# FFN up products on seeded sums in one whole-PSUM tile, with wide eviction and the last product one group later

## The chip, the cores and the metric

The kernel runs on one core of one Trainium2 chip. The metric is the device time of one execution in microseconds (us), the median of several runs. A core has five engines that work beside each other, each through its own queue in order: PE (TensorE, matmuls into PSUM), DVE (VectorE), ACT (ScalarE), POOL (GpSimd) and SP (SyncE, which here issues the DMAs). PSUM has eight banks of 128 x 512 numbers of 32 bits.

## The reference

One transformer layer for 1024 tokens of width 1024: a mixed attention and a recurrent (RWKV-7) branch, a gated merge and an output projection with a residual, and then the feed-forward part, which is where most of the change lies:

```python
def _conv_ffn(h, w_up, conv_w, w_down):
    u = h @ w_up
    u = lax.conv_general_dilated(u, conv_w[:, None, :], window_strides=(1,),
                                 padding=((CONV_WIDTH - 1, 0),),
                                 dimension_numbers=('NWC', 'WIO', 'NWC'),
                                 feature_group_count=u.shape[-1])
    a, b = jnp.split(u, 2, axis=-1)
    return (jax.nn.silu(a) * b) @ w_down
...
    x = x + y @ w_out[l]
    x = x + _conv_ffn(_rms_norm(x, norm_ffn[l]), ffn_up[l], ffn_conv[l], ffn_down[l])
```

`w_up` is 1024 x 5632, so `a` and `b` have 2816 = 22 x 128 columns each. The convolution has three taps along the tokens, one set per column.

## The kernel before, in words

Activations lie transposed: 128 features on the partitions, tokens along the free axis, in two halves of 512 tokens (half 0, half 1). Every large product is made from 16-bit parts: a 32-bit operand is split into a high part (ACT, a copy to 16 bits) and a low part (the rest, on DVE or POOL), and a product is the three matmuls high x high, high x low and low x high for each of the blocks of 128 along the contraction. Weights are scaled by 256 (`WS`) before the split; the convolution's weights carry 1/256.

The program is written with a tile framework: it places the tiles, sets the semaphores, and orders each engine's queue when the program is built, by priority and by a simulated time line. That order is fixed on the chip. A tile whose buffer is taken again waits until its former users are done; a new pool that lands on the bytes of closed pools waits, in the kernel before, for all the users of those pools. PSUM is eight tiles of one bank, drawn by `ps(tag)` (L214) from four pairs of banks P, M, A, B.

The stages, in order of time: normalization, projections and attention with fill-in projections (to about 620 us); the RWKV part, unit by unit, with dense fill-ins (to about 970), among them the output projection of half 0 (`wout0`, L822), its normalization `norm0` (L841) and the up part of half 0 for the first feature groups (`ffn0`, L868, i = 0 to 5); then half 1: projection, normalization, and the up part of half 1 for i = 0 to 5 (loop at L1618). In that loop, `wslot` (L1590) loads and splits weights, `taps` (L1512) evicts a bank, with ACT for the first tap and DVE for the two shifted ones, the first tokens of half 1 taking two columns of half 0 from `cvl`; `silu` (L1522) makes tanh on ACT and two gate steps on DVE and stores `th_d`. Beside it `tprep` (L1538) makes the 16 sums of normalized rows (T1 to T4) that the next stage needs; the rows of half 0 are there only as 16-bit pairs, and `summed` adds these up again.

For i = 6 to 21 both halves are done together in the loop at L1670 ("group" below). Its 2 x 2 block product (two halves of the contraction and a, b by two token halves) is made with seven products of 12 matmuls each in place of eight (Strassen's scheme in Winograd's form), on sums of weights and sums of rows. `prep_up` (L1600) prepares the next group's weights in four steps: load both raw tiles and scale them on ACT (`wraw`, L1573), split `a`; sums `s12` on DVE and their split; sums `s34` and their split; split of the second half of `b`. `split8` (L1580) takes the high part on ACT and the low part on POOL. The results are put together by five DVE sums over PSUM and two kept tiles (p1, q, u2); four evictions of 512 columns follow (L1688 to L1697), then two gates.

The down part follows (L1702 to the end), with the same kind of products; its weights pass `wraw` and `slot` (L1727).

The change and the prediction touch, by line: L81 (`HT`, tags of half 0's normalized rows), L178 to L184 (pools), L214 (`ps`), L841 (`norm0`), L1116 to L1121 (pools of the RWKV stage), L1507 to L1696 and L1727. L261 is the low part of `wload`, used by all the earlier weights; L271 and L291 are matmuls of the plain products, L1649 those of the grouped ones, L1759 and L1830 those of the down part.

## Time and profile before

| What | us |
|---|---|
| median of 3 runs (lowest, highest) | 1735.83 (1735.3, 1738.83) |
| the profiled execution, its own time | 1733.72 |
| its span, first to last instruction | 1731.9 |
| PE busy in it | 1646.6 |
| DVE busy | 1247.6 |
| ACT busy | 941.2 |
| POOL busy | 453.0 |
| first matmul of the grouped up products starts | 1180.4 |
| last row of them in the time line starts | 1510.66 |

The profile is of one execution. Matmuls are pipelined, so a busy PE is not a PE at its peak: the count of matmuls in a stretch says more than its busy time. In rows of groups, `out<-in` are the program's tile names without numbers; "count | busy us, mean ns | idle before" follow. In the chain of waits each row is a start, a length, and the engine, tile and line that the chain runs over there. PEld is the loading of weights, SPq the DMA issues of SP's queue.

### The profile page before, as it was taken

The page shows a single profiled execution, that of the slowest core. Times are in us where ns is not written, and L with a number is a line of the kernel's source. Part 1 is how long each engine was busy: PE and PEld are TensorE (multiplying, and loading weights), DVE is VectorE, ACT ScalarE, POOL GpSimd, SP SyncE. Part 2 cuts the span into 40 slices and gives each one's busy share as a digit, 9 for nine tenths or more (in the row PEclk, how much of TensorE's full clock was granted, in tenths as well). Part 3 has the DMA queues.
Part 4 walks back from the last instruction along what each step waited for, and adds up shares of the span by engine and source line. Part 5 has one row for each costly group of instructions (what it writes and reads, how often), then busy time and mean ns, then how long its engine had stood idle before and what let it go on. Part 6 is the DMA issues. An engine that isn't in the chain of part 4 may idle for free.

```text
span 1731.9 us, 30712 instructions
## 1 busy us (share of the span) xinstructions
PE 1646.6 (95%) x11856; PEld 862.9 (50%) x11856; DVE 1247.6 (72%) x2202; ACT 941.2 (54%) x1669; POOL 453.0 (26%) x350
## 2 busy tenths in 40 slices
PE   8999999999999999998999899998998999999998
PEld 3455555555555545675665444443443343444443
DVE  6446577778876656945447595698988888886799
ACT  6665675657667735446445563664544444546430
POOL 1101131121112210000103201103443333556756
PEclk9999999999999999999999999999999999999999
DMA  5342243242444465335455754443222222534402
GB/s 201 112 137 93 85 152 106 80 141 59 130 146 138 126 224 173 124 120 177 135 183 173 272 177 146 141 141 113 92 91 74 73 74 73 185 132 134 134 13 109
DMA packets 124691, 224.66 MB, mean 130 GB/s; under 512 B 16384, under 2 KB 45440, under 8 KB 124416
## 3 DMA queue, kind: packets, MB, share of 16 engines
q1 hardware_dynamic: 124544, 222.69, 39.0%
q8 instruction: 93, 1.52, 0.4%
q14 instruction: 54, 0.44, 0.1%
HBM read 153.86 MB, written 63.96 MB: 126 GB/s over the span
## 4 chain that ended last, share of the span: by engine, by line
PE 37%; DVE 19%; DMA 6%; ACT 5%; issue 3%; SPq 0%; POOL 0%; DVEq 0%; ACTq 0%
PE psP L271 10%; DVE u L1517 4%; DVE th L1527 3%; DMA wraw<-f_up 3%; PE psA L271 2%; PE psP L291 2%; PE psM L1759 1%; PE psP L1759 1%; PE psB L1759 1%; PE psM L1649 1%; PE psA L1759 1%; PE psM L271 1%; PE psP L1830 1%; DMA zs<-sg_d 1%; PE psA L1649 1%
## 5 line engine op out<-in xcount | busy, mean ns | idle before, releaser
L271 PEld LDWEIGHTS <-whi 128*128 128x128 f16 x1840 | 176.9, 98 | 209.7 <-issue 12.1
L271 PE MATMUL psP<-hlo,whi 128*128 128x512 f16 x560 | 212.2, 379 | 2.1 <-DVE hlo L246 2.1
L271 PE MATMUL psP<-hhi,whi 128*128 128x512 f16 x560 | 212.3, 379 | 2.0 <-ACT ad L973 1.5
L261 DVE SCALAR_TENSOR_TENSOR wlo<-wraw,whi 128x1024 f16<-128x1024 f32 (+1 forms) x98 | 112.0, 1143 | 62.5 <-ACT whi L259 38.2
L1577 ACT ACTIVATE wraw<-wraw 128x1024 f32<-128x1024 f32 x66 | 69.7, 1056 | 141.5 <-DMA wraw<-f_up 96.3
L664 DVE TENSOR_TENSOR pl<-pf,ph 128x512 f16<-128x512 f32 (+3 forms) x208 | 117.9, 577 | 36.0 <-ACT pf L663 35.3
L271 PE MATMUL psP<-hhi,wlo 128*128 128x512 f16 x560 | 142.3, 381 | 0.0
L259 ACT ACTIVATE whi<-wraw 128x1024 f16<-128x1024 f32 (+1 forms) x98 | 92.8, 949 | 90.5 <-PE psP L271 46.5
L271 PEld LDWEIGHTS <-wlo 128*128 128x128 f16 x920 | 88.0, 98 | 100.0 <-issue 4.3
L662 ACT ACTIVATE ph<-psA 128x512 f16<-128x512 f32 (+3 forms) x208 | 99.6, 479 | 63.7 <-PE psA L657 32.8
L599 DVE TENSOR_REDUCE mp<-psM 128x1 f32<-128x512 f32 (+2 forms) x192 | 96.0, 516 | 36.2 <-PE psM L597 27.1
L1585 POOL TENSOR_TENSOR wlo<-wraw,whi 128x1024 f16<-128x1024 f32 (+1 forms) x33 | 58.2, 1765 | 162.1 <-ACT whi L1584 146.8
L663 ACT ACTIVATE pf<-psA 128x512 f32<-128x512 f32 (+3 forms) x208 | 100.3, 482 | 0.0
L1527 DVE SCALAR_TENSOR_TENSOR th<-th,u 128x512 f32<-128x512 f32 x38 | 69.1, 1818 | 0.5
L1384 POOL TENSOR_TENSOR b<-b,bonus 128x512 f32<-128x512 f32 x8 | 10.5, 1317 | 217.1 <-ACT b L1382 189.1
L686 POOL TENSOR_TENSOR onat<-onat,ot 128x256 f32<-128x256 f32 x32 | 27.5, 863 | 140.2 <-DVE ot L685 107.2
L672 PEld LDWEIGHTS <-pl 128*128 128x128 f16 x592 | 55.9, 99 | 16.4 <-DVE pl L664 7.1
L667 PEld LDWEIGHTS <-ph 128*128 128x128 f16 x592 | 56.1, 97 | 16.1 <-ACT ph L662 3.1
L1649 PEld LDWEIGHTS <-whi 128*128 128x128 f16 x384 | 38.0, 99 | 49.2 <-issue 5.4
L1585 POOL TENSOR_TENSOR s34l<-s,s34h 128x1024 f16<-128x1024 f32 x16 | 34.6, 2164 | 101.1 <-ACT s34h L1584 101.1
L670 PEld LDWEIGHTS <-ph 128*128 128x128 f16 x592 | 56.2, 98 | 6.1 <-issue 1.9
L1649 PEld LDWEIGHTS <-s34h 128*128 128x128 f16 x256 | 25.7, 100 | 56.0 <-issue 29.2
(707 smaller groups left out, 4612.9 us busy)
## 6 DMA issues: line engine op xcount, KB each, us to landing
wraw<-f_up SPq DMA_DIRECT2D x56, 512.0 KB, 3.3
wraw<-w_t SPq DMA_DIRECT2D x46, 512.0 KB, 3.8
wraw<-f_dn SPq DMA_DIRECT2D x22, 512.0 KB, 3.8
th_d<-th SPq DMA_DIRECT2D x38, 256.0 KB, 2.1
sg_d<-zs SPq DMA_DIRECT2D x32, 256.0 KB, 2.6
wraw<-w_out SPq DMA_DIRECT2D x16, 512.0 KB, 3.3
z_d<-zs SPq DMA_DIRECT2D x28, 256.0 KB, 2.8
x<-xT SPq DMA_DIRECT2D x24, 256.0 KB, 5.8
```

Of the source, the lines that this page charges most:

```text
L259: A.activation(hi[:, :nk], raw, AF.Copy, scale=WS)
L261: V.scalar_tensor_tensor(lo[:, :nk], raw, WS, hi[:, :nk], op0=ALU.mult, op1=ALU.subtract)
L271: lastm[0] = T.matmul(ps, a[:, k], ks_(b, k), start=(n == 0), stop=(n == 3 * nk - 1)).ins
L599: V.reduce_max(mp[:, x, br, t:t + 1], pm[:, 0:(b1 - b0) * 128], axis=AX.X)
L662: A.activation(ph[0:nkey, rg], pa[0:nkey, rg], AF.Exp, scale=0.125)
L663: A.activation(pf[0:nkey, rg], pa[0:nkey, rg], AF.Exp, scale=0.125)
L664: V.tensor_sub(pl[0:nkey, rg], pf[0:nkey, rg], ph[0:nkey, rg])
L1517: V.scalar_tensor_tensor(u[:, d:512], pj[:, 0:512 - d], cw_, u[:, d:512], op0=ALU.mult, op1=ALU.add)
L1527: V.scalar_tensor_tensor(th, th, 0.5, ub, op0=ALU.mult, op1=ALU.mult)
L1577: A.activation(raw, raw, AF.Copy, scale=WS)
L1585: e.tensor_sub(lo[:, ks], raw[:, ks], hi[:, ks])
L1649: T.matmul(bank, w[wi][:, o_ + k], xs_[k][xi], start=start and n == 0, stop=n == 11, skip_group_check=True)
```

## The change

1. All pools get `reuse_waits="tile"`: a tile in a new pool waits only for the users of earlier tiles on its own bytes, not for all the users of the closed pools there.
2. PSUM is one tile of 4096 columns, and `ps` gives slices of 512 columns of it.
3. `norm0` keeps half 0's normalized rows in 32 bits: four in place in the residual tiles, four in a new pool g0; the 16-bit parts of the last two rows move to that pool. `tprep` reads these rows where it added pairs.
4. In the half-1 loop (i < 6) the tap of the first two columns becomes one add of a product made ahead (`edge`); weights whose low part DVE takes aren't scaled first, since the scale is part of the split; the first two are scaled on POOL.
5. `prep_up`: no scaling of raw weights, sums on POOL, low parts on DVE with the scale in the same operation; s12 and s34 splits have two buffers.
6. The loop of groups: ACT copies a partial sum into another bank, and the next product adds to it there (`start=False`); two full sets of four banks by turns; eviction over 1024 columns, both halves at once, so that no tap of half 0's last columns is needed; the last product with its eviction, gate and store (`last`) comes after the second product of the next group.
7. In the down part, the tags and buffers that follow from this.

```diff
-        pp = pool("ps", 1, PSUM)
+        pall = pool("ps", 1, PSUM).tile([128, 4096], F32, name="pall")
...
-            return pp.tile([128, 512], F32, name="ps" + tag, tag=f"bank{b[-1]}", bufs=1)
+            return pall[:, 512 * b[-1]:512 * b[-1] + 512]
...
+                src = t
+                if k < 4:
+                    t = FP["g"].tile([128, 512], F32, name=f"g0_{k}", tag=f"g0_{k}")
+                h2g[k] = t
...
-                    V.scalar_tensor_tensor(t, t, P("norm_ffn", k), rs, op0=ALU.mult, op1=ALU.mult)
+                    V.scalar_tensor_tensor(t, src, P("norm_ffn", k), rs, op0=ALU.mult, op1=ALU.mult)
...
+            V.tensor_tensor(edge[:, :, :, 0], cvl[:, :, :, 1], cw1, op=ALU.mult)
+            V.tensor_tensor(edge[:, :, :, 1], cvl[:, :, :, 0], cw2, op=ALU.mult)
+            V.tensor_add(edge[:, :, :, 0], edge[:, :, :, 0], edge[:, :, :, 1])
+            V.tensor_tensor(edge[:, :, :, 1], cvl[:, :, :, 1], cw2, op=ALU.mult)
...
-                if h:
-                    V.scalar_tensor_tensor(u[:, 0:d], prev(d), cw_, u[:, 0:d], op0=ALU.mult, op1=ALU.add)
+            if h:
+                V.tensor_add(u[:, 0:2], u[:, 0:2], edge[:, i, o])
...
-            t1 = diff(1, f12, summed(0, k), "fu")
+            t1 = diff(1, f12, h2g[k], "fu")
...
-            t4 = diff(4, summed(0, k + 4), t2, "yx")
+            t4 = diff(4, h2g[k + 4], t2, "yx")
...
+            if e is G:
+                lasts[0] = A.activation(hi[:, ks], raw[:, ks], AF.Copy).ins
+                G.tensor_sub(lo[:, ks], raw[:, ks], hi[:, ks])
+            else:
+                lasts[0] = A.activation(hi[:, ks], raw[:, ks], AF.Copy, scale=WS).ins
+                V.scalar_tensor_tensor(lo[:, ks], raw[:, ks], WS, hi[:, ks], op0=ALU.mult, op1=ALU.subtract)
...
         def prep_up(i):
-            ra, rb = wraw(D["f_up"][i]), wraw(D["f_up"][22 + i])
+            ra, rb = ((fp, wp)[i % 2].tile([128, 8, 128], F32, name="wraw", bufs=2) for _ in range(2))
+            load(ra, D["f_up"][i])
+            lastw[0] = load(rb, D["f_up"][22 + i]).ins
             w = {"a": split8(ra, wp, wp, "whi", "wlo", bufs=2)}
+            s12, s34 = (fp.tile([128, 8, 128], F32, name=n_) for n_ in ("s12", "s34"))
+            G.tensor_add(s12[:, lo4], rb[:, lo4], rb[:, hi4])
+            G.tensor_sub(s12[:, hi4], s12[:, lo4], ra[:, lo4])
             yield w
...
+            w["12"] = split8(s12, fp, fp, "s12h", "s12l", bufs=2)
+            G.tensor_sub(s34[:, lo4], ra[:, lo4], rb[:, lo4])
+            G.tensor_sub(s34[:, hi4], ra[:, hi4], s12[:, hi4])
+            yield
+            w["34"] = split8(s34, fp, fp, "s34h", "s34l", bufs=2)
...
+        def taps2(o, i, c):
+            ci = 22 * o + i
+            u = wide(f"U{o}")
+            A.activation(u, c, AF.Copy, scale=P("conv", 88 + ci))
+            for d in (1, 2):
+                V.scalar_tensor_tensor(u[:, d:1024], c[:, 0:1024 - d], P("conv", 44 * (2 - d) + ci), u[:, d:1024],
+                                       op0=ALU.mult, op1=ALU.add)
+            return u
...
+        def last(i, w, ua, cc):
+            b0 = cc[:, 0:512]
+            prod(b0, w["b"], 4, TB[4], False)
+            ub = taps2(1, i, cc)
+            th = wide("TH")
+            t_ = A.activation(th, ua, AF.Tanh, scale=0.5).ins
+            V.scalar_tensor_tensor(th, th, 1.0, ua, op0=ALU.add, op1=ALU.mult)
+            V.scalar_tensor_tensor(th, th, 0.5, ub, op0=ALU.mult, op1=ALU.mult)
+            for h in range(2):
+                nc.sync.dma_start(th_d[h][i], th[:, H[h]])
+            return t_
...
-            pa, pb, pc, pd_ = ps("P"), ps("M"), ps("A"), ps("B")
-            prod(pa, w["a"], 0, b11, True)
-            p1 = tmp("p1", "zs", NZS)
-            A.activation(p1, pa, AF.Copy)
-            prod(pb, w["12"], 4, TB[2], True)
-            u2 = tmp("u2", "fu", 3)
-            V.tensor_add(u2, pb, p1)
-            prod(pa, w["a"], 4, b21, False)
+            ca, cb_ = (pall[:, b_:b_ + 1024] for b_ in (1024 * (i % 2), 2048 + 1024 * (i % 2)))
+            a0, a1, b0, b1 = ca[:, 0:512], ca[:, 512:1024], cb_[:, 0:512], cb_[:, 512:1024]
+            prod(a0, w["a"], 0, b11, True)
+            A.activation(b0, a0, AF.Copy)
+            prod(b1, w["12"], 0, TB[1], True)
+            p5 = fp.tile([128, 512], F32, name="p5")
+            A.activation(p5, b1, AF.Copy)
+            if pend:
+                t_ = last(*pend)
+            prod(b0, w["12"], 4, TB[2], False)
+            A.activation(a1, b0, AF.Copy)
             wn = next(g_)
-            prod(pc, w["12"], 0, TB[1], True)
-            q = tmp("q", "fu", 3)
-            V.tensor_add(q, pc, p1)
+            prod(a0, w["a"], 4, b21, False)
             next(g_)
-            prod(pb, w["34"], 0, TB[3], False)
-            V.tensor_add(pd_, pb, q)
...
+            prod(b0, w["34"], 0, TB[3], False)
+            u3 = fp.tile([128, 512], F32, name="u3")
+            A.activation(u3, b0, AF.Copy)
+            V.tensor_add(b1, b1, u3)
+            prod(a1, w["34"], 4, b22, False)
+            V.tensor_add(a1, a1, p5)
+            pend = i, w, taps2(0, i, ca), cb_
             next(g_)
```

More of the change, by code (lines that the diff above doesn't have):

```diff
@@ L180, in pool @@
                 kw["space"] = space
-            return stack.enter_context(tc.tile_pool(name=name, bufs=bufs, **kw))
+            return stack.enter_context(tc.tile_pool(name=name, bufs=bufs, reuse_waits="tile", **kw))
         cp = pool("cst")
-        pp = pool("ps", 1, PSUM)
+        pall = pool("ps", 1, PSUM).tile([128, 4096], F32, name="pall")
         wp = pool("w")
@@ L323, in build @@
         cvl = cp.tile([128, NE, 2, 2], F32, name="cvl")
+        edge = cp.tile([128, NE, 2, 2], F32, name="edge")
         km_d = dr.tile([4, 128, S], F32, name="km_d")
@@ L839, in wout0 @@
                 ob["sq7"] = sq
+        h2g = [None] * 8
         def norm0():
@@ L852, in norm0 @@
             for n, k in enumerate(NK):
-                hi[k], lo[k] = (FP["h"].tile([128, 512], F16, name=f"h2{c}0_{k}", tag=HT[2 * n + x]) for x, c in enumerate("hl"))
+                hi[k], lo[k] = (FP["g" if n > 5 else "h"].tile([128, 512], F16, name=f"h2{c}0_{k}", tag=HT[2 * n + x])
+                                for x, c in enumerate("hl"))
                 if k > 3:
@@ L1507, in build @@
             tc.cur_priority = pe_ + 20000
+            cw1, cw2 = (par[:, o_:o_ + 44].rearrange("p (o i) -> p i o", o=2)[:, 0:NE]
+                        for o_ in (PAR["conv"][0] + 44, PAR["conv"][0]))
+            V.tensor_tensor(edge[:, :, :, 0], cvl[:, :, :, 1], cw1, op=ALU.mult)
+            V.tensor_tensor(edge[:, :, :, 1], cvl[:, :, :, 0], cw2, op=ALU.mult)
+            V.tensor_add(edge[:, :, :, 0], edge[:, :, :, 0], edge[:, :, :, 1])
+            V.tensor_tensor(edge[:, :, :, 1], cvl[:, :, :, 1], cw2, op=ALU.mult)
         yst.close()
@@ L1510, in build, with taps @@
         fp = pool("ffn", 1, stack=fst)
-        def taps(u, o, i, h, pj, prev):
+        def taps(u, o, i, h, pj):
             ci = 22 * o + i
@@ L1533, in utile @@
         def utile(o, h):
[L1534 removed]
+            return fp.tile([128, 512], F32, name=f"u{o}{h}", tag=f"U{o}", bufs=2)
         TB = [[None] * 4 for _ in range(5)]
         def tprep(k):
[L1539 to L1542 removed]
             def split(j, t):
@@ L1571, in build, with wraw, wslot @@
         rn_ = [3]
-        def wraw(src):
+        def wraw(src, scale="A"):
             rn_[0] += 1
-            raw = (wp, fp)[rn_[0] // 2 % 2].tile([128, 8, 128], F32, name="wraw", bufs=2)
+            x_ = rn_[0] // 2 % 2
+            raw = (wp, fp)[x_].tile([128, 8, 128], F32, name="wraw", bufs=2)
             lastw[0] = load(raw, src).ins
-            A.activation(raw, raw, AF.Copy, scale=WS)
+            if scale == "A":
+                A.activation(raw, raw, AF.Copy, scale=WS)
+            elif scale == "G":
+                G.tensor_scalar(raw, raw, WS, 0.0, op0=ALU.mult, op1=ALU.add)
             return raw
         def split8(raw, ph, pl, th, tl, ks=slice(0, 8), e=None, **kw):
-            e = e or G
             hi = ph.tile([128, 8, 128], F16, name=th, **kw)
             lo = pl.tile([128, 8, 128], F16, name=tl, **kw)
-            lasts[0] = A.activation(hi[:, ks], raw[:, ks], AF.Copy).ins
-            e.tensor_sub(lo[:, ks], raw[:, ks], hi[:, ks])
+            if e is G:
[4 more added lines that the diff above has]
+                V.scalar_tensor_tensor(lo[:, ks], raw[:, ks], WS, hi[:, ks], op0=ALU.mult, op1=ALU.subtract)
             return hi, lo
         wn_ = [0]
-        def wslot(src, ks=slice(0, 8)):
+        def wslot(src):
             n = wn_[0] % 4
@@ L1635, in build @@
                     run(mm3(pj, hi, lo, h2hi[1], h2lo[1], 8))
-                lasts[0] = taps(u, o, i, 1, pj, lambda d: cvl[:, i, o, 2 - d:2])
+                lasts[0] = taps(u, o, i, 1, pj)
                 us.append(u)
@@ L1663, in build, with wide @@
                     load(acc[m, h], x2_d[h][m])
-        def tmp(name, tag, n):
-            return FP["f"].tile([128, 512], F32, name=name, tag=tag, bufs=n)
+        def wide(name):
+            return fp.tile([128, 1024], F32, name=name, tag=name, bufs=2)
+        def taps2(o, i, c):
[6 more added lines that the diff above has]
+            return u
@@ L1680, in build @@
             wn = next(g_)
-            prod(pc, w["12"], 0, TB[1], True)
-            q = tmp("q", "fu", 3)
-            V.tensor_add(q, pc, p1)
+            prod(a0, w["a"], 4, b21, False)
             next(g_)
-            prod(pb, w["34"], 0, TB[3], False)
-            V.tensor_add(pd_, pb, q)
-            u = [[utile(o, h) for h in range(2)] for o in range(2)]
-            taps(u[0][0], 0, i, 0, pa, None)
-            prod(pc, w["34"], 4, b22, False)
+            prod(b0, w["34"], 0, TB[3], False)
@@ L1696, in build @@
-            t_ = taps(u[1][0], 1, i, 0, pb, None)
-            taps(u[1][1], 1, i, 1, pd_, lambda d: pb[:, 512 - d:512])
-            silu(i, 0, u[0][0], u[1][0])
-            silu(i, 1, u[0][1], u[1][1])
             w = wn
+        t_ = last(*pend)
         for m in range(4, 8):
@@ L1731, in slot @@
                 return [wp.tile([128, 8, 128], F16, name=t, bufs=2) for t in ("whi", "wlo")]
-            return [fp.tile([128, 8, 128], F16, name=t) for t in (("s12h", "s12l"), ("s34h", "s34l"))[n // 2]]
+            return [fp.tile([128, 8, 128], F16, name=t, bufs=2) for t in (("s12h", "s12l"), ("s34h", "s34l"))[n // 2]]
         def cut(dst, src, e):
```

34 lines of the change are left out of this document (10 added, 24 removed).

## The prediction, made before the changed kernel was timed

> **What bounds the kernel now.** I read the page first, then a table of busy time by stretches, then who PE waits for, then the chain of waits.
>
> ```profile
> span 1731.9 us, 30712 instructions
> ...
> PE 37%; DVE 19%; DMA 6%; ACT 5%; issue 3%; SPq 0%; POOL 0%; DVEq 0%; ACTq 0%
> ```
>
> ```profile
> 1180.41:1200.00 19.59, 13.35 (x51) 5.26 (x50) 19.20 (x33) 10.96 (x16) 6.63 (x3) 0.83 0.51 183
> 1200.00:1280.00 80.00, 80.00 (x372) 36.26 (x371) 67.76 (x106) 40.30 (x55) 34.74 (x18) 1.00 0.25 86
> 1280.00:1500.00 220.00, 198.88 (x881) 87.63 (x879) 188.65 (x263) 102.39 (x142) 84.71 (x44) 0.97 0.23 79
> ...
> 1100.00:1180.41 80.41, 80.41 (x373) 36.37 (x372) 76.18 (x119) 58.22 (x80) 10.85 (x4) 1.00 0.38 128
> 1514.98:1690.00 175.02, 175.02 (x811) 79.24 (x810) 136.95 (x191) 85.95 (x139) 113.28 (x85) 1.00 0.31 104
> ...
> 780.00:1000.00 220.00, 201.47 (x2100) 120.36 (x2099) 121.01 (x219) 116.11 (x204) 37.12 (x26) 0.97 0.58 192
> ```
>
> The columns are the stretch, its length, then busy time and instructions of PE, PEld, DVE, ACT and POOL, then the granted clock, DMA share and GB/s. The rewritten loop (i = 6 to 21, seven products each) runs from 1180.4 to about 1515. Its pace when nothing holds it is in the second row: 372 matmuls in 80.00 us, 0.215 us each, so 84 matmuls of one group are 18.1 us. Against that pace 1180 to 1200 loses 19.59 - 51 x 0.215 = 8.6 us, and 1280 to 1500 loses 220 - 881 x 0.215 = 30.6 us; the rows between, before (1100 to 1180) and after lose nothing. So **39 us** can be had at most here, and after 1515 PE is full again, so what the loop saves reaches the end. PE's own waits name the two places:
>
> ```profile
> PE psA L1649 <- DVE q L1683: 20.1, 10, 2.5
> PE psA L1649 <- ACT T1h L1547: 4.3, 1, 4.3
> ```
>
> That is one stall per group behind the sum q, and one big stall at the entrance. Why DVE is late is shown by the chain of waits over one group (start, length, what):
>
> ```profile
> 1299.72 1.06 ACT wraw L1577
> 1300.78 0.58 ACT u L1514
> 1301.38 0.76 DVE u L1517
> ...
> 1314.43 2.38 DVE th L1527
> 1316.83 0.33 SPq L1528
> 1317.24 3.50 DMA wraw<-f_up
> 1320.83 1.06 ACT wraw L1577
> ```
>
> PE is not on it. The chain closes on itself in 1320.83 - 1299.72 = **21.1 us**: DVE finishes th, SP can store it, only then issues the next weight load queued behind that store, ACT stands still in its queue at the scaling of that load (L1577), the tap copies behind it are late, and DVE starts late. Part of DVE's 15 us there is waiting inside an instruction. The timeline first, then DVE's groups in 1280 to 1490 (count | busy us, mean ns | idle before):
>
> ```profile
> 1311.59 2.13 POOL L1585 TENSOR_TENSOR wlo<-wraw,whi 128x1024 f16<-128x1024 f32 x1 [5.54 <-ACT whi L1584]
> ...
> 1311.87 2.39 DVE L1527 SCALAR_TENSOR_TENSOR th<-th,u 128x512 f32<-128x512 f32 x1
> ...
> 1313.68 2.57 POOL L1585 TENSOR_TENSOR s12l<-s,s12h 128x1024 f16<-128x1024 f32 x1
> ```
>
> ```profile
> L1527 DVE SCALAR_TENSOR_TENSOR th<-th,u 128x512 f32<-128x512 f32 x20 | 47.2, 2359 | 0.3
> ...
> L1517 DVE SCALAR_TENSOR_TENSOR u<-psB,par,u 128x511 f32<-128x511 f32 (+1 forms) x20 | 15.0, 750 | 20.4 <-ACT u L1514 20.0
> ...
> L1526 DVE SCALAR_TENSOR_TENSOR th<-th,u 128x512 f32<-128x512 f32 x20 | 12.8, 677 | 0.0
> L1691 DVE TENSOR_TENSOR psA<-psA,u 128x512 f32<-128x512 f32 x10 | 6.9, 690 | 0.0
> ```
>
> The same shape takes 677 ns at L1526 and 2359 at L1527, where a POOL operation runs from start to nearly the end. L1517, with one operand in PSUM, stays at 750.
>
> **The change part by part.** Other prices, from the same kind of view (ACT in 1280 to 1490; POOL and DVE, whole span, shapes apart):
>
> ```profile
> L1577 ACT ACTIVATE wraw<-wraw 128x1024 f32<-128x1024 f32 x20 | 21.1, 1057 | 80.0 <-DMA wraw<-f_up 63.6 <-DMA wraw<-f_dn 15.8
> ...
> L1584 ACT ACTIVATE whi<-wraw 128x1024 f16<-128x1024 f32 x10 | 10.4, 1040 | 0.0
> L1514 ACT ACTIVATE u<-psM,par 128x512 f32<-128x512 f32 x10 | 6.9, 687 | 0.0
> ...
> L1584 ACT ACTIVATE whi<-wraw 128x512 f16<-128x512 f32 x10 | 6.2, 620 | 0.0
> L1675 ACT ACTIVATE p<-psP 128x512 f32<-128x512 f32 x10 | 5.9, 586 | 0.0
> ```
>
> ```profile
> L935 POOL TENSOR_TENSOR lw<-cum,lw 128x512 f32<-128x512 f32 x8 | 10.5, 1313 | 91.5 <-DVE cf L676 38.4 <-DVE cum L934 32.5 <-PE psA L657 20.6
> ```
>
> ```profile
> L261 DVE SCALAR_TENSOR_TENSOR wlo<-wraw,whi 128x1024 f16<-128x1024 f32 x74 | 94.1, 1271 | 43.1 <-ACT whi L259 18.9 <-PE psP L271 15.8 <-issue 6.0
> ...
> L261 DVE SCALAR_TENSOR_TENSOR wlo<-wraw,whi 128x512 f16<-128x512 f32 x24 | 17.9, 747 | 19.4 <-ACT whi L259 19.4
> ```
>
> Another 512 columns cost DVE 1271 - 747 = 524 ns and ACT 1040 - 620 = 420.
>
> *DVE, per group.* Gone: five sums, four weight sums (to POOL), eight 512-wide taps, four small ones, four 512-wide gate steps. Come: two sums 2 x 0.690, four taps of 1023 columns 4 x (0.750 + 0.524), two gate steps 2 x (0.677 + 0.524), three low parts of 1024 and one of 512, 3 x 1.271 + 0.747. Sum 1.4 + 5.1 + 2.4 + 4.6 = **13.4 us**, where now it is 188.65/220 x 21.1 = 18.1.
>
> *ACT, per group.* The two raw scalings go (2.1 us, and with them the place where ACT stood for 80 us). Come four copies, 2 x 1.107 for wide taps, one wide tanh, the splits as before: 4 x 0.586 + 2.2 + 1.04 + 3.74 = 9.3 us, now 9.8. Copies whose output is in PSUM (the two seeds) have no row; between nothing and a tap's 0.687, I take the copy's 0.586, the nearest; both ends change ACT by 1.2 us at most, under its 9 us of slack.
>
> *POOL, per group.* Four sums of 512, 4 x 1.313 = 5.3 us, for 84.71/220 x 21.1 = 8.1 now.
>
> *PE, per group.* Still 84 matmuls, 18.1 us. The new order puts at least one product (12 x 0.215 = 2.6 us) between a product and the one that needs its copy: the seed of b0 has two products to hide under (5.2 us), the seed of a1 one (2.6 us, against 0.586 and one ACT split of 1.04 ahead of it). The last product of a group, with its b taps, tanh, gate and store, moves behind the second product of the next. If the cover of the a1 seed is gone (two splits ahead, 0.586 + 2.08 against 2.6), PE loses tenths of a microsecond.
>
> *The closed chain.* Store and load still share SP's queue, and a load can still stand behind a store that waits for DVE. But what first touches the raw weights now is POOL, then a split: behind the load come 2 x 1.313 on POOL and 1.04 on ACT before a tap copy can be held. Round: tap copy 1.1, two taps 2.5, gate 2.4, two stores 0.7, load 3.5, POOL 2.6, split 1.0, **13.8 us** plus whatever DVE does in between. The remaining DVE work is 13.4 - 4.9 = 8.5; if half of it lies in between, the round is 18.1, just PE's own. So I expect PE as the bound with a small leak: nothing in the first five groups, as now, and 0.5 us in each of the other eleven, 5.5 us. Ends: 0, and the whole 8.5 in between, 22.3 (first rival).
>
> [...] DVE operations with two SBUF operands (gate, low parts: 7.0 us) now meet 5.3 us of POOL instead of 8.1. Worst, DVE waits for all of it: 18.7 us a group, 0.6 above PE. That fits in the leak. [...]
>
> *The entrance (1180 to 1200).* DVE comes in with a backlog (its groups in 1120 to 1197):
>
> ```profile
> L1541 DVE TENSOR_TENSOR zs<-h2h,h2l 128x512 f32<-128x512 f16 x8 | 5.5, 684 | 0.1
> ...
> L1519 DVE SCALAR_TENSOR_TENSOR u<-cvl,par,u 128x1 f32<-128x1 f32 x12 | 4.3, 361 | 0.0
> ```
>
> Rows kept in 32 bits remove the eight sums, 5.5 us. Of 24 small taps 12 adds and 4 products remain; at the 0.2 us of an unblocked one that is 3.2 for 8.3 us (4.3 and 4.0 for the other width). Four weight sums (2.7) leave, four low parts (4.6) come. Net about 9 us less backlog; I leave 4 of the 8.6 us lost, since T1 is now needed by the second product. Ends 0 and 8.6.
>
> *norm0* writes four rows to a new tile instead of in place: no instruction more. The ten ACT scalings before the splits of i < 6 go; PE is full there (row 1100 to 1180), so this earns nothing.
>
> *One PSUM tile, per-tile waits, all through the kernel.* No instruction changes. Per-tile waits can open early starts; the trace has one candidate on the chain of waits, the load for the second solve:
>
> ```profile
> 683.92 4.78 DMA AD<-ad_d
> ```
>
> Later, 780 to 1000 leaves PE idle for 220 - 201.47 = 18.5 us. PE is full between, so an earlier start earns only what it removes there: between 0 and, say, two thirds, 12; I take 2. The ends also hold reordering losses of the same size.
>
> Sum: 39 - 4 - 5.5 = 29.5 in the loop, 2 elsewhere. The profiled execution took 1733.72 us (its span and 1.8 around it), the median shown is 1735.83. 1733.7 - 31.5 = 1702.2, and 2.1 more on the scale of the median: **1704 us**.
>
> **Rivals.**
>
> 1. *The round through SP stays the bound.* If DVE order puts all its work between taps and store, 22.3 us would be no gain; between that and 18.1, 20 us for eleven groups loses 21 + 4 instead of 9.5: 1704 + 15.5 = **1720**. For: today PE isn't on the chain at all. Against: ACT's head-of-queue stall is gone. 20%.
>
> 2. *Freed waits pay too.* No leak and 10 us from 780 to 1000: 1704 - 5.5 - 8 = **1690**. For: the load at 683.92, late in its stage. Against: PE is full till 780. 16%.
>
> 3. *The other side: banks in program order.* With one PSUM tile a bank's users follow each other as written. Fill-in projections and query projections share two banks in the attention part; a fill-in written after a query projection may no longer run before it:
>
> ```profile
> 371.00:416.00 45.00, 12.62 (x57) 5.39 (x56) 1.00 0.25 72
> ```
>
> This row of busy time counts the projections' line alone (L271): 12.6 us of PE in 45 us. If held out in three such stretches, PE loses 38 us; decides if more than 31.5 us of it is not made up later: **1742** with the loop's gain only. Against: fill-ins already run nearly in written order, and they are needed anyway. 7%.
>
> 4. *The change doesn't do what it says:* seeds and wide reads hold banks so long that PE waits at every seed, 16 x 2 x 1 us, with the stalls of today gone: 1704 + 32 = **1736**. Against: two full sets of banks, used in turn. 4%.
>
> 5. *Matmuls closer than 0.215 us.* Then DVE's 13.4 us would bound, 16 x (18.1 - 13.4) = 75 us less: **1629**. Against: 372 in 80.00 us with no idle. 1%. [...]
>
> **How the numbers follow.** Forecast 52%, the rivals 20, 16, 7, 4, 1. The forecast's own range is 1696 to 1712. To leave out no more than 2 in 10 the range takes in rivals 1 and 2 with the bounds of entrance and reordering: **1687 to 1726**. About 0.2%, 3.5 us, is what a measurement here can tell from no change. Faster 52 + 20 + 16 + 1, less 2 for a first rival at its worst: 0.87; same 0.05 (rival 4 and that worst); slower 0.08.
>
> **What would show it.** Right: groups 18.1 to 18.6 us apart, over 81 matmuls in 18 us in 1280 to 1480, no PE wait on a DVE sum, PE on the chain there, DVE near 13 to 16 us a group, gate steps of 1.2 us with a few at 2.5. Entrance: idle under 4 us. Wrong: groups 20 us apart with DMA f_up and th on the chain (rival 1); PE idle in 100 to 620 up by 10 us or more (rival 3); PE waiting for a seed copy in each group (rival 4).

## The result and the profile after

The changed kernel takes 1717.8 us (median of 4 runs, 1715.58 to 1723.3), the kernel before, on the same chip, 1737.33 (4 runs, 1735.3 to 1739.86). The ratio is 0.9879, 95% interval 0.9859 to 0.99: about 20 us faster, where the prediction had 31.8. The profiled execution took 1718.12 us.

The span and the engines' shares of the chain that ended last, from the page of the changed kernel:

```profile
span 1716.1 us, 30297 instructions
...
PE 37%; DVE 11%; DMA 7%; ACT 6%; issue 5%; POOL 5%; SPq 0%; DVEq 0%; POOLq 0%; ACTq 0%
```

Busy time by stretches of the changed kernel (stretch, length, PE, PEld, DVE, ACT and POOL with instructions, granted clock, DMA share, GB/s):

```profile
780.00:1000.00 220.00, 201.23 (x2045) 120.23 (x2044) 117.99 (x214) 110.88 (x196) 37.84 (x26) 0.94 0.57 187
...
1180.41:1200.00 19.59, 14.54 (x57) 5.93 (x56) 18.12 (x26) 8.54 (x14) 9.83 (x6) 0.83 0.49 172
1200.00:1280.00 80.00, 80.00 (x372) 36.21 (x371) 58.20 (x49) 37.13 (x47) 26.51 (x17) 1.00 0.25 87
1280.00:1480.00 200.00, 194.43 (x887) 86.51 (x886) 144.31 (x125) 94.04 (x121) 60.31 (x38) 1.00 0.25 87
1280.00:1500.00 220.00, 210.90 (x956) 93.67 (x955) 156.83 (x138) 108.50 (x141) 74.46 (x47) 0.99 0.30 105
```

From 1280 to 1500 PE does 956 matmuls where it did 881. At the pace of the stretch from 1200 to 1280 (80.00 / 372 = 0.215 us) it still loses 220 - 956 x 0.215 = 14.5 us there; it lost 30.6. The entrance is hardly better: 19.59 - 57 x 0.215 = 7.3 us lost, before 8.6. From 780 to 1000 PE is as busy as before (201.23 us, before 201.47). PE's own waits (in all, times, longest):

```profile
PE pall L1668 <- ACT pall L1723: 7.9, 11, 3.6
...
PE pall L1668 <- ACT T4h L1557: 5.1, 1, 5.1
```

The stall behind a sum on DVE has gone; in its place stands the copy that seeds a1 (L1723), ten times 0.43 us and once 3.65. That longest one is in the last group. The timeline there, ACT and then PE (start, length, engine, line, out and in; in brackets the idle time before):

```profile
1478.86 1.06 ACT L1589 ACTIVATE wraw<-wraw 128x1024 f32<-128x1024 f32 x1 [0.71 <-DMA wraw<-f_dn]
1479.83 0.61 ACT L1601 ACTIVATE whi<-wraw 128x512 f16<-128x512 f32 x1
1480.34 1.09 ACT L1690 ACTIVATE U<-pall,par 128x1024 f32<-128x1024 f32 x1
1481.34 1.66 ACT L1772 ACTIVATE hhh<-thr 128x512 f16<-128x512 f32 x3
1482.90 0.58 ACT L1723 ACTIVATE pall<-pall 128x512 f32<-128x512 f32 x1
```

```profile
1483.53 0.38 PE L1668 MATMUL pall<-T3h,s34h 128*128 128x512 f16 x1 [3.65 <-ACT pall L1723]
...
1484.26 0.63 PE L1668 MATMUL pall<-T3l,s34h 128*128 128x512 f16 x1
```

Two things that the other groups don't have stood on ACT ahead of the copy for which PE waited: the scaling of a weight of the down part (L1589), with the wait for its load 1.7 us, and three splits for the down part (L1772), 1.6 us. With the usual 0.43 they make the 3.65. After the stall PE ran some eight matmuls 0.43 us apart, half its pace.

Where the time came from is best read by number of matmul, since both kernels have the same matmuls, nearly in the same order. From the starts of the matmuls in the traces: how many us earlier than in the kernel before PE starts its n-th matmul. The groups begin at matmul 9529.

```
n                          9500   9590   9700  10830  10950  11570
time in the kernel before  1174   1203   1226   1501   1526   1660
lead of the changed one    -0.8    0.5    0.5   22.3   16.8   16.8
```

So what lies before the groups gives nothing in the end (-0.8), the entrance 1.3 us, the groups 21.8, and the end of the loop takes 5.5 back. (The spans differ by 15.8; the last 1.0 us of the lead goes behind matmul 11570.) On the way the lead was 4.8 us at 780 and gone by 1000. That can't be put down to the change: the kernel of run 6 below, whose engines do the same as in the kernel before up to 1150 us, led by 2.1 us at 780 and was 1.8 behind at 1000.

The first five groups stand 18.13 us apart, but for the stall at the entrance; then the distance is 18.57 once and 19.02 or 19.03 nine times. That second number has a chain of its own. The chain of waits of the changed kernel over one group (start, length, what):

```profile
1381.88 1.07 ACT TH L1703
...
1384.12 0.70 DVE wlo L1602
...
1384.83 3.55 DMA wraw<-f_up
...
1388.54 1.43 POOL s L1624
1389.97 2.21 POOL s L1628
1392.18 1.24 POOL s L1625
...
1393.44 1.07 ACT s12h L1601
...
1394.53 1.31 DVE s12l L1602
1395.84 0.61 DVE pall L1730
1396.45 0.61 DVE pall L1732
...
1397.09 1.12 ACT U L1690
...
1398.69 2.22 issue
1400.92 1.07 ACT TH L1703
```

Again PE isn't on it, and it closes in 1400.92 - 1381.88 = **19.04 us**: tanh and first gate step, then the low part of b's second half, which frees a raw buffer, the load into it, three weight sums on POOL, the split of s12, the two sums in PSUM that stand behind its low part on DVE, the wide copy, its taps (the "issue" row), the next tanh. PE needs 18.13; the first five groups run ahead of the round, until that lead is used up. The copy for which PE then waits is only the place where this round meets PE.

### The profile page after: what moved, and what is told of

Read it like the earlier page. It is cut to its first block, busy times and chain, and to the rows that moved or that the text cites. A ratio compares the mean times of both kernels' runs of the same rounds, so it can differ in the third digit from the quotient of the medians.

```text
span 1716.1 us, 30297 instructions
## 1 busy us (share of the span) xinstructions
PE 1645.0 (96%) x11856; PEld 864.0 (50%) x11856; DVE 1194.7 (70%) x1978; ACT 917.1 (53%) x1625; POOL 433.0 (25%) x352
## 4 chain that ended last, share of the span: by engine, by line
PE 37%; DVE 11%; DMA 7%; ACT 6%; issue 5%; POOL 5%; SPq 0%; DVEq 0%; POOLq 0%; ACTq 0%
PE pall L271 15%; PE pall L1796 5%; PE pall L1867 4%; DMA wraw<-f_up 2%; PE pall L1668 2%; POOL s L1628 2%; PE pall L291 2%; DMA zs<-sg_d 1%; POOL s L1624 1%; DVE s12l L1602 1%; PE pall L1220 1%; POOL s L1625 1%; DMA np_d<-zs 1%; ACT U L1690 1%; DVE wlo L1602 1%
## 5 line engine op out<-in xcount | busy, mean ns | idle before, releaser
L271 PEld LDWEIGHTS <-whi 128*128 128x128 f16 x1840 | 177.1, 98 | 211.8 <-issue 14.5
L271 PE MATMUL pall<-hlo,whi 128*128 128x512 f16 x608 | 229.6, 379 | 2.1 <-DVE hlo L246 2.1
L271 PE MATMUL pall<-hhi,whi 128*128 128x512 f16 x608 | 229.1, 379 | 2.0 <-ACT ad L981 1.5
L271 PE MATMUL pall<-hhi,wlo 128*128 128x512 f16 x608 | 154.7, 382 | 0.0
L663 ACT ACTIVATE ph<-pall 128x512 f16<-128x512 f32 (+3 forms) x208 | 99.6, 479 | 63.3 <-PE pall L658 31.5
L600 DVE TENSOR_REDUCE mp<-pall 128x1 f32<-128x512 f32 (+2 forms) x192 | 95.9, 516 | 34.7 <-PE pall L598 26.4
L664 ACT ACTIVATE pf<-pall 128x512 f32<-128x512 f32 (+3 forms) x208 | 100.0, 481 | 0.0
L1692 DVE SCALAR_TENSOR_TENSOR U<-pall,par,U 128x1023 f32<-128x1023 f32 x64 | 82.0, 1282 | 11.1 <-ACT U L1690 9.1
L1624 POOL TENSOR_TENSOR s<-wraw 128x512 f32<-128x512 f32 x16 | 25.6, 1602 | 219.4 <-DMA wraw<-f_up 206.2
L1601 ACT ACTIVATE s12h<-s 128x1024 f16<-128x1024 f32 x16 | 16.9, 1057 | 99.5 <-POOL s L1625 99.5
L668 PEld LDWEIGHTS <-ph 128*128 128x128 f16 x592 | 56.1, 97 | 15.7 <-ACT ph L663 2.5
L1798 DVE SCALAR_TENSOR_TENSOR acc<-pall,acc 128x512 f32<-128x512 f32 x80 | 52.1, 680 | 10.4 <-PE pall L1796 10.3
L1668 PE MATMUL pall<-h2h,whi 128*128 128x512 f16 x128 | 49.5, 387 | 5.1 <-ACT T4h L1557 5.1
```

Of the source, the lines that this page charges most:

```text
L271: lastm[0] = T.matmul(ps, a[:, k], ks_(b, k), start=(n == 0), stop=(n == 3 * nk - 1)).ins
L600: V.reduce_max(mp[:, x, br, t:t + 1], pm[:, 0:(b1 - b0) * 128], axis=AX.X)
L663: A.activation(ph[0:nkey, rg], pa[0:nkey, rg], AF.Exp, scale=0.125)
L664: A.activation(pf[0:nkey, rg], pa[0:nkey, rg], AF.Exp, scale=0.125)
L1668: T.matmul(bank, w[wi][:, o_ + k], xs_[k][xi], start=start and n == 0, stop=n == 11, skip_group_check=True)
L1692: V.scalar_tensor_tensor(u[:, d:1024], c[:, 0:1024 - d], P("conv", 44 * (2 - d) + ci), u[:, d:1024], op0=ALU.mult, op1=ALU.add)
```

## The experiments

All times beside the kernel before, on the same chip. The stage before the groups is nearly the same work in all of them, yet the lead at matmul 9500 ran from 2.0 to -5.7 us from profile to profile. So each run is read by the lead that it adds from there (1174 us in the kernel before) to matmul 11570. For the changed kernel that is 16.82 + 0.84 = 17.7 us.

```
                          median   ratio (95% interval)     9500   9590   9700  10830  11570   added
changed kernel            1717.8   0.9879 (0.9859-0.9900)   -0.8    0.5    0.5   22.3   16.8    17.7
seed_a1_first             1710.58  0.9847 (0.9822-0.9873)   -5.6   -3.6   -3.6   20.3   19.3    24.9
both_seeds_first          1701.93  0.9803 (0.9777-0.9829)   -2.3   -0.3   -0.4   30.0   30.0    32.2
drain_after_seed          1715.3   0.9878 (0.9857-0.9900)    1.1    2.8    2.8   24.6   20.6    19.5
first_group_other_banks   1718.74  0.9894 (0.9864-0.9924)   -0.7    4.7    0.3   21.8   16.5    17.2
old_weight_prep           1726.75  0.9930 (0.9909-0.9951)   -3.9   -4.7   -4.7    9.6    7.6    11.5
new_prep_alone            1706.03  0.9823 (0.9808-0.9839)   -1.8   -2.4   -2.4   27.9   27.2    29.0
half0_rows_summed         1724.11  0.9925 (0.9909-0.9941)    2.0   -2.4   -2.4   19.5   12.8    10.8
pool_wide_waits           1719.74  0.9895 (0.9878-0.9911)   -4.2   -3.1   -3.1   18.6   13.5    17.6
last_in_own_group         1727.58  0.9934 (0.9914-0.9954)   -0.8    0.8   -1.4    7.6    7.6     8.4
first_groups_low_on_pool  1727.08  0.9931 (0.9912-0.9951)   -5.7   -9.9   -9.9   11.1    6.9    12.6
three_fixes               1704.58  0.9803 (0.9786-0.9820)   -0.8    2.0    2.0   32.3   32.3    33.1
entrance_sums_first       1700.39  0.9769 (0.9743-0.9794)   -4.4    4.6    2.0   32.3   32.3    36.7
```

**1. The seed of a1 ahead of b's taps.**

```diff
-            if pend:
-                t_ = last(*pend)
+            if pend:
+                prod(pend[3][:, 0:512], pend[1]["b"], 4, TB[4], False)
             prod(b0, w["12"], 4, TB[2], False)
-            A.activation(a1, b0, AF.Copy)
+            seed = A.activation(a1, b0, AF.Copy).ins
+            if pend:
+                t_ = last(*pend, seed)
```

(`last` without its product; its wide copy is issued behind `seed`.)

> In the changed kernel groups from the sixth on are 19.03 us apart where seven products of 12 matmuls at 0.216 us make 18.13; 0.6 us of it is lost ahead of the T3 product, which waits for the copy that seeds a1. This copy stands in ACT's queue behind the wide copy of b's taps. Here the copy of the taps is issued behind the seed. Theory 1 (order of ACT's queue): the ten PE waits for this seed go, groups come to 18.4 us, and the end comes 5 to 6 us earlier than in the changed kernel, span about 1710.5. Theory 2 (a round through DVE, SP and POOL sets the pace, first rival of the prediction): the wait goes but another one takes its place, groups stay at 19.0 and the span within 1.5 us of 1716.

Between the two. The lead added is 24.9 us, some 7 more than in the changed kernel, but 4.5 of that come behind matmul 10830, at the end of the loop. The later groups are 18.4 to 19.7 us apart, and another wait took over (waits of PE, 1150 to 1520):

```profile
PE pall L1668 <- ACT pall L1715: 3.8, 7, 1.0
PE pall L1668 <- ACT pall L1722: 0.8, 1, 0.8
```

L1715 is the seed of b0. The chain of waits over its groups still runs through the load, POOL's sums and tanh. So the a1 seed alone wasn't what set the pace.

**2. Both seeds first.** As above, and the wide copy of the a taps comes behind the next group's seed of b0:

```diff
-            A.activation(b0, a0, AF.Copy)
+            s0 = A.activation(b0, a0, AF.Copy).ins
+            if pend:
+                pend[2] = taps2(0, pend[0], pend[2], s0)
...
-            pend = i, w, taps2(0, i, ca), cb_
+            pend = [i, w, ca, cb_]
```

> As the run before, and the copy that seeds b0 is also issued ahead of the wide copy of the a taps, which waits for a sum on DVE; 0.3 us per group are lost at that place now. Theory 1 (order of ACT's queue): groups at 18.13 us from first to last, PE without a wait between the entrance and the last group, 0.9 us less in each of ten groups, span about 1707. Theory 2 (the round through SP): no faster than the run before; groups above 18.8 us.

As theory 1 has it: every group 18.13 us after the one before. The stretch 1280 to 1480 of this run, and below it what the chain of waits holds from 1360 to 1400:

```profile
1280.00:1480.00 200.00, 200.00 (x928) 90.71 (x927) 157.98 (x130) 105.00 (x129) 70.12 (x43) 1.00 0.29 102
```

```profile
by line: PE pall L1668 100.4%
```

928 matmuls in 200 us, none of it idle, and PE alone on the chain. The end of the loop, where the changed kernel gave 5.5 us back, costs nothing. One caution: the edit also put the last split of raw weights (L1601) ahead of tanh (L1702) on ACT, as the timeline of this run shows:

```profile
1375.57 0.63 ACT L1601 ACTIVATE whi<-wraw 128x512 f16<-128x512 f32 x1 [1.13 <-PE pall L1668]
1376.11 1.04 ACT L1702 ACTIVATE TH<-U 128x1024 f32<-128x1024 f32 x1
```

In the changed kernel tanh and the first gate step come ahead of that split and its low part, which is a link of the 19.04 us round. Whether it was this or the seed of b0 that opened the round, these runs don't separate. That a round through the load must set the pace (the prediction's first rival) is refuted: load, store and sums are all still there.

**3. The down part's splits behind the last seed.**

```diff
-                    with tc.issue_after(t_) if i0 == 2 else ExitStack():
+                    with tc.issue_after(t_ if i0 == 2 else seed) if i0 < 4 else ExitStack():
```

> In the last group the seed of a1 stands behind two splits of stored rows for the down part, and PE waits 3.65 us and then runs ten matmuls at half pace. Here those splits are issued behind the last seed. Theory 1 (order of ACT's queue at the hand-over): the 3.65 us wait falls below 1.2 us and 4 us are won at the end, span about 1712. Rival: the splits are needed so early that the down part starts late; then PE loses the same 4 us ten us later and the span stays at 1715 to 1717.

Half. The long wait falls to 2.2 us, not below 1.2, and some 2 us are won. What is left beyond the usual 0.43 is the scaling of the down-part weight, which still stands ahead of the seed (ACT's timeline in this run):

```profile
1476.61 1.06 ACT L1589 ACTIVATE wraw<-wraw 128x1024 f32<-128x1024 f32 x1 [0.81 <-DMA wraw<-f_dn]
```

With both seeds first, and no hold on these splits, the wait has gone.

**4. Other banks for the first group.**

```diff
-            ca, cb_ = (pall[:, b_:b_ + 1024] for b_ in (1024 * (i % 2), 2048 + 1024 * (i % 2)))
+            ca, cb_ = (pall[:, b_:b_ + 1024] for b_ in (1024 * (1 - i % 2), 2048 + 1024 * (i % 2)))
```

> The two sets of banks change parity for a: group 6 takes two banks for a that the half-1 loop left a feature group earlier. Theory 1 (banks): the 5.05 us of PE idle at 1184 to 1189 are the wait of the first product for DVE's last taps on its bank; with other banks it runs at once, the idle goes and 3 to 5 us are won, span about 1712. Theory 2 (DVE's backlog): the first product runs at once, but PE then waits for the low part of T1 and T2, which DVE makes at 1194 to 1196 in either case; at most 1.5 us are won, span 1714.5 to 1716.5.

The first product ran at once, and at matmul 9590 the run was 5.4 us better than at 9500, the changed kernel 1.3. But PE had two other waits, and at matmul 9700 only 1.0 us was left. ACT's and PE's timeline in this run:

```profile
1188.27 0.63 ACT L1557 ACTIVATE T4h<-t 128x512 f16<-128x512 f32 x1 [1.23 <-DVE t L1563]
1189.04 0.63 ACT L1540 ACTIVATE th<-u 128x512 f32<-128x512 f32 x1
1189.58 0.58 ACT L1716 ACTIVATE pall<-pall 128x512 f32<-128x512 f32 x1
...
1200.74 1.06 ACT L1601 ACTIVATE s12h<-s 128x1024 f16<-128x1024 f32 x1 [4.58 <-POOL s L1625]
1201.70 0.58 ACT L1723 ACTIVATE pall<-pall 128x512 f32<-128x512 f32 x1
```

```profile
1190.21 0.38 PE L1668 MATMUL pall<-T2h,s12h 128*128 128x512 f16 x1 [3.19 <-ACT pall L1716]
...
1202.33 0.59 PE L1668 MATMUL pall<-T3h,s34h 128*128 128x512 f16 x1 [2.79 <-ACT pall L1723]
```

The first product had ended at about 1184; its seed stood behind a split that waited for DVE. The seed of a1 then stood behind the split of the next group's weight sums, which waited for POOL; that wait, and seven matmuls at half pace behind it, gave the win back. Neither theory named these waits, though the second had the sum nearly right: a wait was there whichever bank was free.

**5. Weights prepared as before, in the new loop.** Raw weights scaled on ACT, sums on DVE, low parts on POOL.

```diff
+            e_ = G if i < 22 else None
+            if e_ is G:
+                for r_ in (ra, rb):
+                    A.activation(r_, r_, AF.Copy, scale=WS)
...
-            G.tensor_add(s12[:, lo4], rb[:, lo4], rb[:, hi4])
+            V.tensor_add(s12[:, lo4], rb[:, lo4], rb[:, hi4])
...
-            w["12"] = split8(s12, fp, fp, "s12h", "s12l", bufs=2)
+            w["12"] = split8(s12, fp, fp, "s12h", "s12l", e=e_, bufs=2)
```

> The changed kernel with the weights of the groups prepared as before: raw weights scaled on ACT, sums of weights on DVE, low parts on POOL; seeds, wide evictions and the late last product stay. Busy time per group by the rows of the two kernels: DVE 13.7 - 5.2 + 2.7 = 11.2 us, ACT 9.0 + 2.1 = 11.1, POOL 8.1, all far under PE's 18.1. Theory 1 (the loss before the change was the chain in which ACT stands at the scaling of a load that itself stood behind a store): that stand comes back, now with the seeds behind it, groups from the sixth on are 20 us or more apart, span 1725 to 1735. Theory 2 (the loss was DVE's load, which sums and evictions made): groups stay at 19.0 or below, span 1710 to 1717.

Theory 1, if less than it said: groups from the fourth on mostly 19.1 to 19.6 us apart and two of 21, 19.6 on average; 11.5 us added in place of 17.7. DVE was busy for only 135.39 of 200 us there, so DVE's load isn't what holds PE.

**6. The new preparation alone, in the kernel before.** Edit 5 of the change without its second buffers, and nothing else: no scaling, sums on POOL at their old place in the program, low parts on DVE.

> The kernel before with nothing changed but the preparation of the groups' weights: no scaling on ACT, sums on POOL, low parts on DVE. Busy time of DVE per group: 18.1 - 2.7 + 4.6 = 20.0 us. Theory 1 (the chain through ACT's scaling): the chain opens, DVE is the bound at 20 us and the span falls to 1717 to 1725 (1.1 us in each of some eleven groups). Theory 2 (DVE's load): DVE has more to do, and groups take 21 us or longer, span 1731 to 1745.

Far better than either theory: 1706.03 us, 29.0 us added, **more than the whole change** (17.7). Stretch 1280 to 1480 of this run, and DVE's second gate step in 1280 to 1490 (count | busy us, mean ns | idle before):

```profile
1280.00:1480.00 200.00, 199.49 (x925) 90.31 (x924) 187.72 (x278) 90.93 (x129) 57.67 (x43) 1.00 0.28 97
```

```profile
L1527 DVE SCALAR_TENSOR_TENSOR th<-th,u 128x512 f32<-128x512 f32 x24 | 22.7, 948 | 0.2
```

PE is full, with DVE at 187.72/200 x 18.13 = 17.0 us a group, not 20.0. The sum of 20.0 took the 18.1 us of before as work; but the gate step that took 2359 ns beside POOL's low parts takes 948 here. Where the groups are concerned, seeds, wide evictions and the late last product weren't needed. One caution: this edit does two things to the old round. It takes the scaling off ACT, and it takes the stretch off two gate steps, which alone is 2 x 1.41 = 2.8 us of a round of 21.1, where PE needs 18.13. How much each is worth no run separates.

**7. Half 0's rows added up again.** Eight sums on DVE ahead of the groups.

```diff
-            t1 = diff(1, f12, h2g[k], "fu")
+            t1 = diff(1, f12, summed(0, k), "fu")
...
-            t4 = diff(4, h2g[k + 4], t2, "yx")
+            t4 = diff(4, summed(0, k + 4), t2, "yx")
```

> The changed kernel with half 0's rows added up from their 16-bit pairs again, eight sums of 0.68 us on DVE ahead of the groups. Theory 1 (DVE's backlog sets the entrance): 5.5 us more on DVE make PE's idle time between 1180 and 1205 larger by 3 to 5.5 us and the span 3 to 6 longer. Theory 2 (they lie under the full PE of 1100 to 1180): idle within 1 us of the changed kernel's 5.05.

Theory 1. Busy time in 1180 to 1205, first this run, then the changed kernel (PE alone):

```profile
1180.00:1205.00 25.00, 15.02 (x56) 6.07 (x57) 23.45 (x28) 10.50 (x15) 11.71 (x8) 0.80 0.34 118
```

```profile
1180.00:1205.00 25.00, 19.95 (x82) 0.86 0.41 139
```

Idle 9.98 against 5.05; between matmuls 9500 and 9590 this run loses 4.4 us and the changed kernel wins 1.3. The rows in 32 bits are worth 5.7 us, about the 5.5 us of DVE that they remove.

**8. Waits for whole pools again.**

```diff
-            return stack.enter_context(tc.tile_pool(name=name, bufs=bufs, reuse_waits="tile", **kw))
+            return stack.enter_context(tc.tile_pool(name=name, bufs=bufs, **kw))
```

> The changed kernel with waits for all users of a closed pool, as before the change, in place of waits per tile. The order of every engine's queue is the same as in the changed kernel, only waits differ. The prediction gave the per-tile waits 2 us. If they do that much, the span is 1718 and the loss lies before 1100 us; if they do nothing, every stage is within what runs of one kernel differ by, and the span is 1714 to 1718; the second rival would have 8 us or more there.

Nothing that can be told from the spread between profiles: -4.2 at matmul 9500 (the changed kernel -0.8, others from 2.0 to -5.7), and 17.6 us added from there, the changed kernel 17.7. Two us before the groups are neither shown nor excluded. The queues hold the same instructions in the same order, so only waits could have differed.

**9. The last product in its own group.**

```diff
-            if pend:
-                t_ = last(*pend)
...
-            pend = i, w, taps2(0, i, ca), cb_
+            t_ = last(i, w, taps2(0, i, ca), cb_)
```

> The changed kernel with the last product, its evictions, gate and store in their own group and not one later. The copy that seeds b0 then has one product (2.6 us) to hide under and not two, and ACT has both wide tap copies ahead of it or around it. Theory 1 (order of ACT's queue): PE waits for the seed of b0 come on top of those for a1, 0.5 to 1 us in each of the later groups, span 1720 to 1728. Theory 2 (the wait is all in the a1 seed, behind b's taps): those taps now come earlier, the a1 waits go, and the span is 1708 to 1714. The prediction held the cover of b0's seed to be what the move is for.

Theory 1. Groups are 19.88 us apart from the second on. PE's waits:

```profile
PE pall L1668 <- ACT pall L1716: 21.3, 14, 2.1
```

1.59 us for the seed of b0 in nearly every group, which now stands behind two wide copies. So the move of the last product is worth 9 us (17.7 - 8.4), as cover for a seed that the change itself brought.

**10. Low parts of the first two groups on POOL.**

```diff
-            w = {"a": split8(ra, wp, wp, "whi", "wlo", bufs=2)}
+            e_ = G if i < 8 else None
+            if e_ is G:
+                for r_ in (ra, rb):
+                    A.activation(r_, r_, AF.Copy, scale=WS)
+            w = {"a": split8(ra, wp, wp, "whi", "wlo", e=e_, bufs=2)}
```

(and `e=e_` in the three other splits)

> The changed kernel with the weights of the first two groups (6 and 7) scaled on ACT and their low parts on POOL, as before the change, sums on POOL too: 4.6 us less on DVE for each. Theory 1 (the low parts that came to DVE eat the relief at the entrance): PE's idle time in 1180 to 1200 falls from 5.05 us to 1 to 3, span 1712 to 1714 against 1716 (runs differ by some us before 1100; counted from there). Theory 2 (the wait is for a bank or a seed alone): idle stays at 4.5 us or above.

Not theory 1. It is one wait for a bank, as in theory 2, but twice as long, 10.72 us, and 4.2 us are lost between matmuls 9500 and 9590. Busy time in 1180 to 1200 of this run:

```profile
1180.00:1200.00 20.00, 9.28 (x41) 3.83 (x39) 13.78 (x14) 9.44 (x14) 19.92 (x13) 0.82 0.39 131
```

POOL is full (19.92 of 20), ACT stands at its splits of POOL's sums with the tap copies behind them, and DVE, with less to do, waits for those. Here work taken off DVE didn't help, since it went to an engine whose results ACT's queue must wait for.

**11. Three fixes together** (2, 3 and 4).

> Both seeds first, the splits of the down part behind the last seed, and the other banks for the first group, together. Theory 1 (order of ACT's queue everywhere): groups at 18.13 us, no PE wait between the entrance and the down part, the entrance as in the run with other banks or 1 us better, span 1700 to 1703 (a spread of 4 us before 1100 comes on top). Rival: the hand-over needs no hold any more when both seeds go first, and the entrance gives nothing: as the run with both seeds, 1703 to 1705.

33.1 us added, 0.9 more than with the seeds alone; the medians of the two runs don't differ by more than their spread. The hold on the splits added nothing that can be seen, as the rival said.

**12. The entrance in another order.** With the three fixes; the last half-1 evictions and gates come behind the first seed and the last four splits:

```diff
             s0 = A.activation(b0, a0, AF.Copy).ins
+            if i == NE:
+                with tc.issue_after(s0):
+                    next(tg[3])
+                    next(tg[3])
+                    for o in range(2):
+                        lasts[0] = taps(us[o], o, NE - 1, 1, pjs[o])
+                silu(NE - 2, 1, *prev)
+                silu(NE - 1, 1, *us)
...
+            if i == NE:
+                prod(a0, w["a"], 4, b21, False)
```

> The run with three fixes, and at the entrance the last half-1 feature group's evictions and gates (i = 4 and 5) come behind the copy that seeds b0 and behind the last four splits of sums of rows, on ACT and on DVE; in group 6 alone the fourth product (rows of half 0 only) is second. Theory 1 (at the entrance too, the order of the queues of ACT and DVE decides): the seed wait of 3.2 us goes, PE's idle time in 1180 to 1205 falls from 4.1 us (in the changed kernel 5.05) to 1.5 to 2.5, and counted from 1143 us the end is 1.5 to 3 us earlier than with three fixes. Theory 2 (DVE has more work there than time): the wait comes back as one for T1's low part or a gate, idle stays above 3.5 us, or the same time is lost in groups 7 and 8.

Theory 1. Busy time in 1180 to 1205 of this run:

```profile
1180.00:1205.00 25.00, 22.71 (x105) 10.05 (x104) 25.00 (x32) 11.29 (x17) 12.71 (x8) 1.00 0.50 167
```

Idle 2.29 us; 36.7 us added, 3.6 more than with three fixes. With 1700.39 us (0.9769 of the kernel before) it has the lowest median of these kernels. DVE has no free moment there (25.00 of 25). Of the idle time 0.6 us are for a low part on DVE; 1.7 are for the seed of a1, which as in run 4 stands behind the split of POOL's sums.

## Why the prediction was right in direction and too large

The time lies within the range only because the range took in the first rival. It is outside the forecast's own 1696 to 1712, and of the signs of being right that the prediction gave, several didn't come: groups stood 19.03 us apart, PE was off the chain there, and the entrance kept 5.05 us of idle time. PE waited for no sum on DVE, as foreseen.

*What bounds the kernel.* Right that a closed chain through the weights' preparation held PE, from DVE's gate over a load to ACT's scaling: in run 6, with the preparation alone changed, PE is full, and in run 5, with the old one in the new loop, the groups come to 19.6 us. Which link of the chain counted isn't shown, the scaling on ACT or the stretched gate step; in run 5 the scaling is back, and the wide gate steps keep their 1226 ns.

*The sums per engine.* Right in size: DVE 144.31/200 x 19.03 = 13.7 us a group (13.4 foreseen), ACT 8.9 (9.3), POOL 5.7 (5.3). The prices held as well, save for the pair shown under "DVE beside POOL". Groups of the changed kernel in 1280 to 1480, DVE, then ACT:

```profile
L1692 DVE SCALAR_TENSOR_TENSOR U<-pall,par,U 128x1023 f32<-128x1023 f32 (+1 forms) x42 | 53.8, 1282 | 8.4 <-ACT U L1690 7.0
...
L1704 DVE SCALAR_TENSOR_TENSOR TH<-TH,U 128x1024 f32<-128x1024 f32 x11 | 13.5, 1225 | 12.9 <-ACT TH L1703 12.9
```

```profile
L1723 ACT ACTIVATE pall<-pall 128x512 f32<-128x512 f32 x10 | 6.0, 597 | 0.0
```

A wide tap takes 1282 ns (1274 estimated), a wide gate step 1225 (1201), the seed copy, which had no row, 597 (586). But such sums don't tell how long a group takes. They were nearly the same in the changed kernel at 19.03 us (DVE 13.7) and with both seeds first at 18.13 (157.98/200 x 18.13 = 14.3).

*The closed chain.* The step that was mis-sized first: "13.8 us plus whatever DVE does in between", with half of DVE's other work, so 18.1 and a leak of 0.5 us in each of eleven groups. The round measures 19.04. It closes elsewhere: not over the store on SP's queue, but over the raw buffer that the last low part frees, with three POOL sums (one at 2.2 us) and the two sums in PSUM on it. The leak is 0.44 us once and 0.9 in nine groups, 8.5 us for 5.5. That is most of the 3.3 us by which the groups fall short (21.8 for 25.1).

*The cover of the seeds.* The prediction gave b0's seed two products to hide under and took the a1 seed's slip for tenths of a microsecond. The slip of the a1 seed was 0.43 us of wait, as foreseen for "two splits ahead"; that of b0's, 0.3 us more a group, wasn't foreseen, nor that the cover would fail in the last group, where a scaling and splits of the down part join ACT's queue. For that hand-over the sum has no term; it cost 5.5 us.

*The entrance.* "I leave 4 of the 8.6 us lost": 7.3 remained by the count of the stretch, 1.3 us were won by the lead instead of 4.6. The 32-bit rows gave what DVE's sums were priced at (run 7). Two waits weren't in the working: fixed banks, so that the first product waits for the last taps on its bank, and the seeds in ACT's queue behind splits that wait for DVE or POOL (run 4). With the order changed, 9.0 us were won between matmuls 9500 and 9590, of which 2.6 went again before 9700 (run 12).

*Elsewhere.* The 2 us for per-tile waits can't be seen (run 8); the kernel came to the groups 0.8 us behind, within what profiles of the same instructions differ by.

Together, in the profiles: 3.3 + 5.5 + 3.3 + 2.8 = 14.9 us, and 1.0 behind matmul 11570; the gain of 15.8 us fell short of 31.5 by 15.7.

*The rivals.* The first (a round longer than PE) was right in kind, at 19.03 for its 20 us, though by another path than SP's store. The fourth (PE waits at the seeds) has the place right and the size wrong: 7.9 us in all. The second and the third didn't come: PE's idle time from 780 to 1000 is unchanged, and PE is within 1 us of the kernel before at 1100. The fifth's condition, matmuls of the groups closer than 0.215 us, no run shows: 372 in 80.00 us again in the changed kernel, 928 in 200.00 with both seeds first.

*DVE beside POOL.* The worst sum, in which gate and low parts wait for all of POOL's 5.3 us and DVE takes 18.7 a group, didn't come (13.7), but the low parts moved to DVE do meet POOL. In the changed kernel's timeline the low part of a raw tile takes 2.29 us: it begins beside one of POOL's sums and ends 1.08 us after it, and the next sum, 2.25 us long where the one behind it takes 1.27, ends 1.13 us after the low part does (DVE and POOL alone):

```profile
1388.53 1.44 POOL L1624 TENSOR_TENSOR s<-wraw 128x512 f32<-128x512 f32 x1 [12.80 <-DMA wraw<-f_up]
1388.76 2.29 DVE L1602 SCALAR_TENSOR_TENSOR wlo<-wraw,whi 128x1024 f16<-128x1024 f32 x1
...
1389.93 2.25 POOL L1628 TENSOR_TENSOR s<-wraw 128x512 f32<-128x512 f32 x1
```

It is one such meeting a group. The low part of s34, with no POOL operation beside it, takes 1208 ns.

## What to carry to other kernels

Where a chain of waits closes on itself, look for the edit that takes a link out, and try it alone first: here moving the weights' preparation gave more than the whole change, whose rewritten loop put new copies for PE into an in-order queue full of others. For each copy that PE waits for, write down what stands ahead of it in its engine's queue and what that waits for, in the first and last turn of the loop above all. After a change work out the length of every closed round, buffers included; the sum of each engine's work says nothing of it.
